# The recurrence's gate blocks in the two 64-row halves of the array, both directions side by side, in place of block-diagonal full blocks

## The chip, the cores and the metric

The kernel runs on one NeuronCore of one Trainium2 chip, as one launch. The metric is the device time of a run in microseconds (us), the median over runs: 1235.79 us for the kernel before (3 runs, 1235.56 to 1236.59). The four engines that compute are called PE (matrix multiply), DVE (vector), ACT (scalar, with table functions) and POOL; SP starts the transfers.

## What is computed

An encoder of two layers over 512 tokens of 1024 channels, all in float32. Each layer normalises its input, projects it with one matrix whose columns are split between eight attention heads (queries, keys, values), the input of a recurrence and its gate branch, joins the attention and the recurrence in an output projection, and ends in a gated MLP. The change touches the gates of the recurrence alone, which the reference writes so:

```python
def rg_lru(x, w_gate, b_gate, lam, reverse):
    bsz, s, _ = x.shape
    xb = x.reshape(bsz, s, N_LRU_BLOCKS, LRU_BLOCK)
    g = jnp.einsum("bsnc,gncd->gbsnd", xb, w_gate).reshape(2, bsz, s, D_LRU)
    g = g.astype(jnp.float32) + b_gate.astype(jnp.float32)[:, None, None, :]
    r_gate = jax.nn.sigmoid(g[0])
    i_gate = jax.nn.sigmoid(g[1])
    log_a = -LRU_C * r_gate * jax.nn.softplus(-lam.astype(jnp.float32))
    a = jnp.exp(log_a)
    u = jnp.sqrt(-jnp.expm1(2.0 * log_a)) * (i_gate * x.astype(jnp.float32))
    return linear_scan(a, u, reverse).astype(x.dtype)
```

There are 512 recurrent channels in 8 blocks of 64 (`N_LRU_BLOCKS`, `LRU_BLOCK`). For each of two directions `d` (forward, backward) and two gates `g` (0: `r_gate`, 1: `i_gate`), each block of 64 channels is multiplied by a 64 x 64 matrix of its own. Two scans along the tokens follow, one in each direction, whose results are added.

## The kernel before

Activations lie with channels on the 128 partitions and the 512 tokens along the row. Each float32 operand is split into a leading part (`h`, `hi`) and a trailing part (`l`, `lo`), and each product is three matmuls (`mm3`, L190 to L192: hi by h, hi by l, lo by h). The weights come as a stream of 205 chunks, each 128 x 1024 (eight blocks of 128 x 128), in the order in which PE takes them (`weight_plan`): SP starts the transfer into `raw`, ACT copies it into `hi` (L173), DVE subtracts to get `lo` (L174). Six chunks are loaded and three are split ahead of use; `hi` and `lo` have four buffers each.

Between the input of the recurrence and the output projection, `MIX` (L43) lists steps: query, key, value and gate-branch tiles (`qps`, `kps`, `vps`, `gate`: 24 matmuls each, from one chunk), the recurrence's convolution (`xc`, split into `xcs_h`, `xcs_l`) and its gates (`lru_gates`, steps t0 to t3), and the attention's scores (`s`), transposes (`ptw`, `pth`) and products (`o`). A scheduler then settles the order on each engine; an engine carries out its instructions in that order, and waits for what the next of them needs. Most of these products land in three banks of `ps_mm`, which are handed round: a product cannot start before the bank's former content has been read. `urgent()` puts the instructions that read a bank ahead of others in the scheduler's eyes.

`lru_gates` (L460) does one tile of 128 channels, four in a layer. For each direction and gate a 128 x 128 block with the two 64 x 64 matrices on its diagonal is multiplied with the tile (three matmuls 128x128x512 into a bank `gp`, whose digits after the name are layer, tile, direction and gate), and one tanh on ACT (L475) reads the whole bank, since sigmoid(z) is 0.5 + 0.5 tanh(z/2). So there are 12 matmuls, four banks and four tanhs a tile. For each direction follow exp, tanh and square on ACT (L478, L479, L481) and two products on DVE (L482, L483); then one square root over both directions (L487, with a load of ACT's function table before and after it), a product (L489), the two scans (L492 forward, L495 backward) and their sum (L497). The eight gate blocks of two tiles are one chunk, so a layer has two gate chunks, at t0 and t2.

Of the kernel before, what the change touches and what calls it, by code (L numbers as in the profile page):

```python
# [30 lines left out]
# query blocks of 8 grid columns: first key column, number of key columns, offset of the bias  # L31
# [3 lines left out]
# products that raise the tensor engine's clock while the first loads are under way  # L35
# [13 lines left out]
def weight_plan():  # L49
    """128 x 128 weight blocks in the order in which the tensor engine takes them, eight a chunk."""  # L50
    plan = []
    for l in range(L):
# [8 lines left out]
        for step in MIX:  # L61
            if step in ("t0", "t0a", "t2", "t2a"):
                t = int(step[1])
                plan.append(("gate", l, [(t + a, dg) for a in range(2) for dg in range(4)]))
            elif step[0] in IN_TILE and step[-1] != "b":
                column("w_in", IN_TILE[step[0]] + int(step[1]))
# [33 lines left out]
def encoder(ctx: ExitStack, tc: tile.TileContext, x_d, w_d, cols_d, bias_d, out_d):  # L100
# [93 lines left out]
    def gemm_group(banks, w, l, k0, nk, ms, rhs, hooks={}, first=0, total=None):  # L194
        """four tiles of the output at once, one step of the contraction after another"""
# [99 lines left out]
    class Stats:  # L295
# [13 lines left out]
        def columns(self, n, ps=None):  # L309
            """mean square + eps and its power of -1/2, token (128 s + p) at [p, s]"""  # L310
# [11 lines left out]
        def rows(self, c, pl=ps_mm):  # L322
            """the column c of token values on every partition"""
# [7 lines left out]
    # the token axis of the grid as columns of rows  # L331
# [9 lines left out]
    class Scaled:  # L341
        """x times a norm's gain, split; the norm's 1/rms is left to the products"""
# [16 lines left out]
    def finish(st, down_blk, h_in, r_in, l):  # L359
        """the last two tiles of the residual and the final norm, one half of the tokens after the other"""  # L360
# [58 lines left out]
    def layer(l, xn):  # L419
        # -- recurrent branch input --  # L420
# [34 lines left out]
        # -- recurrences --  # L455
# [5 lines left out]
        def lru_gates(t, ds):  # L461
            if t % 2 == 0 and 0 in ds:
                pair["c"] = chunk("gate", l, (t, 0))
            if 0 in ds:
                pair["w"], pair["work"] = p_w2.tile([P, 2 * T], F32, tag="w2", name=f"w2{l}{t}"), []
            c, both, work = pair["c"], pair["w"], pair["work"]
            for d in ds:
                w = both[:, d * T:(d + 1) * T]
                ti = big(p_t, "t", f"ti{l}{t}{d}")
# [13 lines left out]
                nc.vector.scalar_tensor_tensor(out=ti, in0=ti, scalar=1.0, in1=xc[t], op0=ALU.add, op1=ALU.mult)  # L483
                work.append((d, a, w, ti))
            if 1 not in ds:
                return
# [389 lines left out]
```

## Time and profile before

| what | value |
|---|---|
| median of 3 runs | 1235.79 us (1235.56 to 1236.59) |
| span of the profiled execution | 1234.5 us |
| PE busy | 1217.1 us (99%), 5694 instructions |
| DVE busy | 764.9 us (62%) |
| ACT busy | 481.8 us (39%) |
| granted TensorE clock | full in all 40 slices of the span |
| moved by DMA | 114.07 MB, mean 92 GB/s |

The durations and times of the trace come from one profiled execution, whose span is 1234.5 us; the median of the runs stands 1.3 us above it. Times within the trace count from the start of the span. The duration given for a matmul includes its way through the array: the pace is the distance between two starts. Matmuls of one kind follow each other while the former ones are still under way, so a "busy" PE may still be held up a little. The steps of `MIX` fall at about 40 to 165 us in layer 0 and 650 to 775 us in layer 1.

### The profile page before, as it was taken

How to read it: one execution, taken by the hardware profiler on the slowest of the kernel's cores; microseconds unless marked ns; L12 is line 12 of the kernel's file. 1: busy time of each engine (PE TensorE's matmuls, PEld its weight loads, DVE VectorE, ACT ScalarE, POOL GpSimd, SP SyncE). 2: the span in 40 equal slices, each digit the busy share in tenths (PEclk: the TensorE clock that was granted, in tenths of full speed). 3: DMA queues.
4: the chain of work that ended last, by engine and by line, in shares of the span. 5: the costliest groups of instructions: out<-in, count | busy, mean ns of one | idle time of the engine just before them, and what ended most of it. 6: DMA issues, size and time to landing. Idle time of an engine off the chain costs nothing.

```text
span 1234.5 us, 14411 instructions
## 1 busy us (share of the span) xinstructions
PE 1217.1 (99%) x5694; PEld 999.0 (81%) x5694; DVE 764.9 (62%) x1217; ACT 481.8 (39%) x701; POOL 23.7 (2%) x50
## 2 busy tenths in 40 slices
PE   9999999999999999999999999999999999999997
PEld 8777878888888888888887777788888888888886
DVE  7998756765544455554659977477555355555454
ACT  6676433432321232332428864344233222233220
POOL 2000000000000000000010000000000000000000
PEclk9999999999999999999999999999999999999999
DMA  7222213232332332333222221133323323323312
GB/s 259 62 86 90 76 42 103 85 103 91 97 103 94 95 102 91 97 103 96 91 85 76 76 86 52 35 122 101 99 90 103 102 87 101 102 87 102 102 52 69
DMA packets 34354, 114.07 MB, mean 92 GB/s; under 512 B 3824, under 2 KB 7024, under 8 KB 34288
## 3 DMA queue, kind: packets, MB, share of 16 engines
q1 hardware_dynamic: 34144, 113.17, 28.6%
q8 instruction: 44, 0.72, 0.2%
q14 instruction: 22, 0.18, 0.1%
q10 hardware_dynamic: 144, 0.00, 0.0%
HBM read 111.06 MB, written 2.10 MB: 92 GB/s over the span
## 4 chain that ended last, share of the span: by engine, by line
PE 93%; DVE 4%; issue 1%; DMA 0%; POOLq 0%; ACT 0%; POOL 0%; DVEq 0%; SPq 0%; ACTq 0%
PE dn L192 7%; PE dn L191 7%; PE dn L190 7%; PE pl L192 6%; PE pa L192 6%; PE pa L190 6%; PE pl L190 6%; PE pl L191 6%; PE pa L191 6%; PE out L190 2%; PE out L192 2%; PE out L191 2%; PE o L648 2%; PE o L653 2%; PE s L600 1%
## 5 line engine op out<-in xcount | busy, mean ns | idle before, releaser
L173 ACT ACTIVATE hi<-raw 128x1024 fp32r<-128x1024 f32 (+1 forms) x205 | 216.2, 1055 | 438.0 <-PE dn L191 158.9
L174 DVE TENSOR_TENSOR lo<-raw,hi 128x1024 fp32r<-128x1024 f32 (+1 forms) x205 | 249.2, 1216 | 138.0 <-ACT hi L173 137.9
L742 DVE TENSOR_TENSOR ua<-pa,g_ffn_rb 128x512 f32<-128x512 f32 x44 | 30.4, 691 | 112.8 <-PE pa L192 112.8
L750 ACT ACTIVATE uc<-uc,cols 128x512 f32<-128x512 f32 x48 | 34.8, 724 | 130.3 <-DVE uc L748 130.1
L751 DVE TENSOR_TENSOR uc<-pl,uc 128x512 f32<-128x512 f32 x44 | 30.4, 691 | 73.7 <-PE pl L192 72.0
L719 DVE TENSOR_TENSOR dns<-dn,g_ffn_rb 128x512 f32<-128x512 f32 x30 | 20.4, 688 | 29.5 <-PE dn L192 29.5
L748 DVE SCALAR_TENSOR_TENSOR uc<-ua,cols,uc 128x511 f32<-128x511 f32 x48 | 36.0, 751 | 1.6
L746 DVE SCALAR_TENSOR_TENSOR uc<-ua,cols,uc 128x511 f32<-128x511 f32 x48 | 35.8, 745 | 0.1
L612 ACT ACTIVATE p<-p,mx 128x192 f32<-128x192 f32 (+1 forms) x64 | 27.5, 431 | 16.6 <-DVE mx L610 16.6
L648 PE MATMUL o<-ptws,v 128*64 128x128 f32 x128 | 27.7, 298 | 0.0
L600 PE MATMUL s<-k,q 128*128 128x192 f32 (+1 forms) x128 | 23.0, 320 | 3.2 <-DVE q L520 2.2
L190 PE MATMUL out<-atth,hi 128*128 128x512 f32 x64 | 25.9, 405 | 0.0
L600 PEld LDWEIGHTS s<-k,q 128*128 128x128 f32 x128 | 19.9, 190 | 7.1 <-issue 4.3
L192 PE MATMUL out<-atth,lo 128*128 128x512 f32 x64 | 25.3, 395 | 0.0
L191 PE MATMUL out<-attl,hi 128*128 128x512 f32 x64 | 25.1, 392 | 0.0
L606 DVE CUSTOM_DVE_ANT_0 p<-s,bias 128x192 f32<-128x192 f32 (+1 forms) x64 | 18.3, 335 | 10.7 <-PE o L648 9.8
L745 DVE TENSOR_SCALAR uc<-ua,cols 128x512 f32<-128x512 f32 x48 | 23.4, 487 | 1.5
L520 DVE TENSOR_TENSOR q<-qps,g_mix_rb 64x256 f32<-64x256 f32 x32 | 20.6, 645 | 2.3 <-PE qps L192 1.8
L720 DVE TENSOR_TENSOR x<-x,dns 128x512 f32<-128x512 f32 x30 | 20.1, 687 | 0.4
L648 PEld LDWEIGHTS o<-ptws,v 128*64 128x64 f32 x128 | 12.2, 135 | 8.0 <-issue 3.9
L450 DVE SCALAR_TENSOR_TENSOR xc<-xrs,cols,xc 128x511 f32<-128x511 f32 (+1 forms) x24 | 17.9, 744 | 0.3
L192 PE MATMUL pl<-xg_g_ffn_4h,lo 128*128 128x512 f32 x44 | 17.1, 390 | 0.0
(918 smaller groups left out, 3475.2 us busy)
## 6 DMA issues: line engine op xcount, KB each, us to landing
raw<-in_w SPq DMA_DIRECT2D x203, 512.0 KB, 3.5
x<-in_x SPq DMA_DIRECT2D x8, 256.0 KB, 6.0
out_y<-out SPq DMA_DIRECT2D x8, 256.0 KB, 2.3
bias<-in_bias SPq DMA_DIRECT2D x8, 224.0 KB, 2.7
raw<-in_w SPq DMA_DIRECT2D x2, 256.0 KB, 3.6
cols<-in_cols SPq DMA_DIRECT2D x1, 164.0 KB, 6.7
cols<-in_cols ACTq DMA_DIRECT2D x1, 4.0 KB, 3.1
```

Source lines behind the costliest of these rows:

```text
L173: nc.scalar.activation(hi[:, sl], raw[:, sl], AF.Copy)
L174: nc.vector.tensor_tensor(out=lo[:, sl], in0=raw[:, sl], in1=f32(hi[:, sl]), op=ALU.subtract)
L190: nc.tensor.matmul(ps, a[0], b[0], start=start, stop=False)
L191: nc.tensor.matmul(ps, a[0], b[1], start=False, stop=False)
L192: nc.tensor.matmul(ps, a[1], b[0], start=False, stop=stop)
L600: nc.tensor.matmul(ps[:, o:o + ROWS * w], qt[:, b % 4 * P:(b % 4 + 1) * P], kt[:, ROWS * kc0:ROWS * (kc0 + w)], start=True, stop=True)
L648: nc.tensor.matmul(o[p0:p0 + 64, s * P:(s + 1) * P], v[i][:, s * P + p0:s * P + p0 + 64], by_head(t1)[:, 2 * (s % 2):2 * (s % 2) + 2, p0 / ...
L742: nc.vector.tensor_tensor(out=ua, in0=pa, in1=rbf[0], op=ALU.mult)
L746: nc.vector.scalar_tensor_tensor(out=c[:, 1:], in0=ua[:, :T - 1], scalar=w[0], in1=c[:, 1:], op0=ALU.mult, op1=ALU.add)
L748: nc.vector.scalar_tensor_tensor(out=c[:, :T - 1], in0=ua[:, 1:], scalar=w[2], in1=c[:, :T - 1], op0=ALU.mult, op1=ALU.add)
L750: nc.scalar.activation(c, c, AF.Gelu_apprx_tanh, bias=col("conv_ffn_b", j, l))
L751: nc.vector.tensor_tensor(out=c, in0=pl_, in1=c, op=ALU.mult)
```

## The change

The four block-diagonal blocks of a tile become two blocks, one for each gate. In such a block the rows 0 to 63 hold channel block s = 0 of the tile and the rows 64 to 127 hold s = 1, and the columns hold both directions side by side: 64 columns for one direction, 64 for the other (`o = 64 * (s ^ d)`). Each of the three products of a gate is now done twice, for the 64 rows of each half `n`, into a bank of its own (`gp` with layer, tile, gate and half as its digits): 12 matmuls a tile as before, each with 64 rows by 128 columns in place of 128 by 128, in the program's text alternating between the two halves.

A bank now holds both directions of one channel block, the forward direction in its own half of the partitions, the backward one in the other half. So each bank is read by two tanhs 64x512 (L485), eight a tile in place of four. All that belongs to the backward direction lies with its two halves swapped: `xc` is copied with swapped halves into `xs` (two copies 64x512 on ACT, L473), and the backward scan's result is copied back into place (two copies 64x512 on ACT, L510) before the sum. Biases and decays are packed to match on the host. The gate blocks of all four tiles of a layer fit in one chunk, which is taken at t0 and held until t3; the stream has 203 chunks in place of 205. The products on DVE stay as many.

```diff
-            if step in ("t0", "t0a", "t2", "t2a"):
-                t = int(step[1])
-                plan.append(("gate", l, [(t + a, dg) for a in range(2) for dg in range(4)]))
+            if step == "t0":
+                plan.append(("gate", l, [(t, g) for t in range(4) for g in range(2)]))
...
-                for g, o in ((0, w), (1, ti)):
-                    ps = psum(ps_o if d and g and not o_ps[0] else ps_mm, f"gp{l}{t}{d}{g}")
-                    mm3(ps, blk(c, 4 * (t % 2) + 2 * d + g), xcs[t], True, True)
...
+            xs = big(p_t, "t", f"xs{l}{t}")
+            halves_ = (slice(0, 64), slice(64, P))
+            for n in range(2):
+                nc.scalar.activation(xs[halves_[n]], xc[t][halves_[1 - n]], AF.Copy)
+            for g, o in ((0, ws), (1, ti)):
+                ps = [psum(ps_o if n and g and not o_ps[0] else ps_mm, f"gp{l}{t}{g}{n}") for n in range(2)]
+                w = blk(c, 2 * t + g)
+                for a, b in ((0, 0), (0, 1), (1, 0)):
+                    for n, rows in enumerate(halves_):
+                        nc.tensor.matmul(ps[n], w[a][rows], xcs[t][b][rows], start=a + b == 0, stop=a == 1)
+                for d in range(2):
                     i = ((l * 2 + d) * 2 + g) * 4 + t
                     with urgent():
-                        nc.scalar.activation(o, ps, AF.Tanh, scale=0.5, bias=half_b[:, i:i + 1])
+                        for n in range(2):
+                            rows = halves_[n ^ d]
+                            nc.scalar.activation(o[d][rows], ps[n][rows], AF.Tanh, scale=0.5, bias=half_b[rows, i:i + 1])
...
-                nc.vector.scalar_tensor_tensor(out=ti, in0=ti, scalar=1.0, in1=xc[t], op0=ALU.add, op1=ALU.mult)
-                work.append((d, a, w, ti))
...
+                nc.vector.scalar_tensor_tensor(out=ti[d], in0=ti[d], scalar=1.0, in1=xs if d else xc[t],
+                                               op0=ALU.add, op1=ALU.mult)
+                work.append((d, a, w, ti[d]))
...
-                    nc.vector.tensor_tensor(out=fb[t], in0=fb[t], in1=w, op=ALU.add)
+                    for n in range(2):
+                        nc.scalar.activation(u[halves_[n]], w[halves_[1 - n]], AF.Copy)
+                    nc.vector.tensor_tensor(out=fb[t], in0=fb[t], in1=u, op=ALU.add)
...
+            o = 64 * (s ^ d)
+            gate[:, :, :, 64 * s:64 * s + 64, o:o + 64] = a["lru_w"][:, d, :, s::2].transpose(0, 2, 1, 3, 4)
```

The scheduler orders the engines anew. In the rows below the numbers behind a name's letters are layer, tile and so on, and what follows the underscore only tells buffers apart. On ACT, in layer 0 around tile 2 of the gates, the order before is this (`p` is the softmax's exponential of scores, `w` and `ti` are the two gates, `w201` is that of tile 1):

```order
L173 ACTIVATE hi13_726<-raw13_695 128x1024
L487 ACT_TABLE_LOAD
L487 ACTIVATE w201_640<-w201_640 128x1024
L612 ACT_TABLE_LOAD
L612 ACTIVATE p034_1168,sm03_1166<-p034_1168,mx03_1165 128x192
L475 ACTIVATE w202_773<-gp0200_775,half_b_165 128x512
L475 ACTIVATE ti020_774<-gp0201_780,half_b_165 128x512
L612 ACTIVATE p034_1168,sm03_1166<-p034_1168,mx03_1165 128x192
L612 ACTIVATE p036_1174,sm03_1166<-p036_1174,mx03_1165 128x192
L475 ACTIVATE w202_773<-gp0210_793,half_b_165 128x512
L612 ACTIVATE p036_1174,sm03_1166<-p036_1174,mx03_1165 128x128
L173 ACTIVATE hi14_767<-raw14_730 128x1024
```

Here the first tanhs of tile 2 come between the exponentials, and the table load and the square root of tile 1 stand well ahead. The same place in the changed kernel:

```order
L626 ACTIVATE p034_1198,sm03_1196<-p034_1198,mx03_1195 128x192 x2
L626 ACTIVATE p036_1204,sm03_1196<-p036_1204,mx03_1195 128x192
L626 ACTIVATE p036_1204,sm03_1196<-p036_1204,mx03_1195 128x128
L499 ACT_TABLE_LOAD
L499 ACTIVATE w201_649<-w201_649 128x1024
L485 ACT_TABLE_LOAD
L485 ACTIVATE w202_785<-gp0200_791,half_b_165 64x512 x2
L485 ACTIVATE w202_785<-gp0201_792,half_b_165 64x512 x2
L510 ACTIVATE ti011_651<-w201_649 64x512 x2
L172 ACTIVATE hi13_744<-raw13_713 128x1024
L290 ACTIVATE xcs0_3h_781<-xc0_3_776 128x512
L473 ACTIVATE xs02_788<-xc0_2_640 64x512
```

All four exponentials, the square root of tile 1 and its two table loads now stand ahead of the first tanhs of tile 2, and behind these come the copies L510 and L473. On PE, in layer 0 where tile 3 of the gates is (`vps00` is the first value tile, `gate00` the first tile of the gate branch), the order before is this:

```order
L190 MATMUL gp0310_969<-xcs0_3h_763,hi11_597 128x512
L191 MATMUL gp0310_969<-xcs0_3l_764,hi11_597 128x512
L192 MATMUL gp0310_969<-xcs0_3h_763,lo11_598 128x512
L191 MATMUL vps00_917<-xg_g_mix0_5l_283,hi14_767 128x512
L192 MATMUL vps00_917<-xg_g_mix0_5h_282,lo14_768 128x512
L190 MATMUL vps00_917<-xg_g_mix0_6h_315,hi14_767 128x512
L191 MATMUL vps00_917<-xg_g_mix0_6l_316,hi14_767 128x512
L192 MATMUL vps00_917<-xg_g_mix0_6h_315,lo14_768 128x512
L190 MATMUL vps00_917<-xg_g_mix0_7h_322,hi14_767 128x512
L191 MATMUL vps00_917<-xg_g_mix0_7l_323,hi14_767 128x512
L192 MATMUL vps00_917<-xg_g_mix0_7h_322,lo14_768 128x512
L190 MATMUL gate00_1007<-xg_g_mix0_0h_170,hi15_818 128x512
```

The fourth bank of the gates, `gp0310`, is filled in the midst of the value tile, with seven of its matmuls between it and `gate00`. The same place in the changed kernel:

```order
L189 MATMUL vps00_938<-xg_g_mix0_7h_322,hi13_744 128x512
L190 MATMUL vps00_938<-xg_g_mix0_7l_323,hi13_744 128x512
L191 MATMUL vps00_938<-xg_g_mix0_7h_322,lo13_745 128x512
L479 MATMUL gp0310_988<-xcs0_3h_781,hi6_338 128x512
L479 MATMUL gp0310_988<-xcs0_3l_782,hi6_338 128x512
L479 MATMUL gp0310_988<-xcs0_3h_781,lo6_339 128x512
L189 MATMUL gate00_1037<-xg_g_mix0_0h_170,hi14_839 128x512
L190 MATMUL gate00_1037<-xg_g_mix0_0l_171,hi14_839 128x512
L191 MATMUL gate00_1037<-xg_g_mix0_0h_170,lo14_840 128x512
L189 MATMUL gate00_1037<-xg_g_mix0_1h_206,hi14_839 128x512
```

The last three gate matmuls, all in the lower half of the rows, now stand directly ahead of `gate00`, behind the whole value tile. On PE, in layer 1 behind tile 1 of the gates (`qps12` is a query tile, `ptw11` and `pth11` the transposes of the second half of a head pair's probabilities), the order before is this:

```order
L190 MATMUL qps12_5132<-xg_g_mix1_0h_4449,hi111_4949 128x512
L191 MATMUL qps12_5132<-xg_g_mix1_0l_4450,hi111_4949 128x512
L627 MATMUL ptw11_5531<-ident_158,p114_5490 128x128
L632 MATMUL pth11_5532<-ident_158,p114_5490 64x128
L627 MATMUL ptw11_5531<-ident_158,p114_5490 128x128
L632 MATMUL pth11_5532<-ident_158,p114_5490 64x128
L627 MATMUL ptw11_5531<-ident_158,p116_5496 128x128
L632 MATMUL pth11_5532<-ident_158,p116_5496 64x128
L627 MATMUL ptw11_5531<-ident_158,p116_5496 128x128
L192 MATMUL qps12_5132<-xg_g_mix1_0h_4449,lo111_4950 128x512
L190 MATMUL qps12_5132<-xg_g_mix1_1h_4458,hi111_4949 128x512
```

The transposes come after two matmuls of the query tile. The same place in the changed kernel:

```order
L191 MATMUL qps12_5180<-xg_g_mix1_5h_4620,lo110_4980 128x512
L641 MATMUL ptw11_5591<-ident_158,p114_5550 128x128
L646 MATMUL pth11_5592<-ident_158,p114_5550 64x128
L641 MATMUL ptw11_5591<-ident_158,p114_5550 128x128
L646 MATMUL pth11_5592<-ident_158,p114_5550 64x128
L641 MATMUL ptw11_5591<-ident_158,p116_5556 128x128 x2
L646 MATMUL pth11_5592<-ident_158,p116_5556 64x128
L189 MATMUL qps12_5180<-xg_g_mix1_6h_4679,hi110_4979 128x512
L190 MATMUL qps12_5180<-xg_g_mix1_6l_4680,hi110_4979 128x512
L191 MATMUL qps12_5180<-xg_g_mix1_6h_4679,lo110_4980 128x512
```

The transposes now come after 18 matmuls of the query tile.

## Rows read from the trace of the kernel before

**Rows 1.** The page, busy time of each engine.
```profile
PE 1217.1 (99%) x5694; PEld 999.0 (81%) x5694; DVE 764.9 (62%) x1217; ACT 481.8 (39%) x701; POOL 23.7 (2%) x50
```
**Rows 2.** The page, the chain that ended last, by engine.
```profile
PE 93%; DVE 4%; issue 1%; DMA 0%; POOLq 0%; ACT 0%; POOL 0%; DVEq 0%; SPq 0%; ACTq 0%
```
**Rows 3.** Waits of PE: us in total, times, longest.
```profile
PE ptw L627 <- DVE p L616: 3.5, 4, 1.5
PE s L600 <- DVE q L520: 2.2, 2, 1.6
```
**Rows 4.** Windows: us; busy (count) of each engine; PE clock; DMA share; GB/s.
```profile
40.00:125.00 85.00, 81.39 (x395) 64.25 (x395) 76.23 (x148) 65.75 (x107) 0.00 (x0) 1.00 0.26 80
125.00:165.00 40.00, 40.00 (x228) 31.07 (x228) 28.95 (x80) 18.21 (x44) 0.00 (x0) 1.00 0.20 65
650.00:735.00 85.00, 81.57 (x401) 65.34 (x401) 76.34 (x153) 65.67 (x110) 0.00 (x0) 1.00 0.26 83
```
**Rows 5.** Timeline of PE at gate tile 3, layer 0: start, us.
```profile
98.13 0.39 PE L190 MATMUL gp<-xcs_3h,hi 128*128 128x512 f32 x1
98.36 0.39 PE L191 MATMUL gp<-xcs_3l,hi 128*128 128x512 f32 x1
```
**Rows 6.** Operations on tiles named gp: ns min/median/max, first and last start, forms.
```profile
L190 PEld LDWEIGHTS gp<-xcs_0h,hi x8: 186/188/188, 40.1 to 650.1; 128*128 128x128 f32 x8
```
**Rows 7.** Timeline of PE, tiles of 64 rows between full ones.
```profile
111.98 0.39 PE L192 MATMUL gate<-xg_g_mix_7h,lo 128*128 128x512 f32 x1
112.30 0.43 PE L648 MATMUL o<-ptws,v 128*64 128x128 f32 x2
112.66 0.32 PE L653 MATMUL o<-pths,v 64*64 64x64 f32 x2
```
**Rows 8.** Groups of instructions on ACT: count, busy us, mean ns, idle before.
```profile
L173 ACT ACTIVATE hi<-raw 128x1024 fp32r<-128x1024 f32 x203 | 214.9, 1059 | 436.8 <-PE dn L191 158.9 <-PE pa L191 154.1 <-issue 30.7
L478 ACT ACTIVATE a<-w,spn 128x512 f32<-128x512 f32 x16 | 12.9, 807 | 0.0
L487 ACT ACT_TABLE_LOAD x8 | 10.3, 1283 | 0.1
```
**Rows 9.** Groups of instructions on DVE, the same columns.
```profile
L719 DVE TENSOR_TENSOR dns<-dn,g_ffn_rb 128x512 f32<-128x512 f32 x30 | 20.4, 688 | 29.5 <-PE dn L192 29.5
L636 DVE COPY pths<-pth 64x384 f32<-64x384 f32 x16 | 8.8, 548 | 8.0 <-PE pth L632 2.8 <-PE o L653 2.6 <-PE ptw L627 2.5
```
**Rows 10.** Timeline of ACT at gate tile 0, layer 0.
```profile
42.54 0.63 ACT L291 ACTIVATE xcs_1h<-xc 128x512 fp32r<-128x512 f32 x1 [0.61 <-DVE xc L450]
43.08 0.67 ACT L475 ACTIVATE ti<-gp,half_b 128x512 f32<-128x512 f32 x1
43.65 0.68 ACT L475 ACTIVATE w<-gp,half_b 128x512 f32<-128x512 f32 x1
```
**Rows 11.** Timeline of ACT at gate tile 2, layer 0.
```profile
79.42 1.28 ACT L612 ACT_TABLE_LOAD   x1 [0.71 <-DVE mx L610]
80.72 0.46 ACT L612 ACTIVATE p<-p,mx 128x192 f32<-128x192 f32 x1
81.23 0.69 ACT L475 ACTIVATE w<-gp,half_b 128x512 f32<-128x512 f32 x1
```
**Rows 12.** Timeline of PE, the starts that the walk compares.
```profile
84.51 0.40 PE L190 MATMUL kps<-xg_g_mix_0h,hi 128*128 128x512 f32 x1
103.57 0.39 PE L190 MATMUL gate<-xg_g_mix_0h,hi 128*128 128x512 f32 x1
673.30 0.33 PE L627 MATMUL ptw<-ident,p 128*128 128x128 f32 x1 [1.45 <-DVE p L616]
```
**Rows 13.** Timeline of DVE at gate tile 3, layer 0.
```profile
98.30 1.29 DVE L489 TENSOR_TENSOR ti<-ti,w 128x512 f32<-128x512 f32 x2
100.64 1.20 DVE L495 TENSOR_TENSOR_SCAN w<-a,ti 128x512 f32<-128x512 f32 x1
104.19 1.16 DVE L539 TENSOR_TENSOR vt<-vps,g_mix_rb 128x512 f32<-128x512 f32 x1
```

More of the change, by code (lines that the diff above doesn't have):

```diff
@@ L459, in layer, with lru_gates @@
         o_ps = [None]
[L461 to L469, printed above, removed]
-                for g, o in ((0, w), (1, ti)):
-                    ps = psum(ps_o if d and g and not o_ps[0] else ps_mm, f"gp{l}{t}{d}{g}")
-                    mm3(ps, blk(c, 4 * (t % 2) + 2 * d + g), xcs[t], True, True)
+        def lru_gates(t):
+            if t == 0:
+                pair["c"] = chunk("gate", l, (0, 0))
+            c = pair["c"]
+            both = p_w2.tile([P, 2 * T], F32, tag="w2", name=f"w2{l}{t}")
+            ws = [both[:, d * T:(d + 1) * T] for d in range(2)]
+            ti = [big(p_t, "t", f"ti{l}{t}{d}") for d in range(2)]
+            xs = big(p_t, "t", f"xs{l}{t}")
[9 more added lines that the diff above has]
+                for d in range(2):
                     i = ((l * 2 + d) * 2 + g) * 4 + t
                     with urgent():
-                        nc.scalar.activation(o, ps, AF.Tanh, scale=0.5, bias=half_b[:, i:i + 1])
+                        for n in range(2):
+                            rows = halves_[n ^ d]
+                            nc.scalar.activation(o[d][rows], ps[n][rows], AF.Tanh, scale=0.5, bias=half_b[rows, i:i + 1])
+            work = []
+            for d in range(2):
+                w = ws[d]
                 i = (l * 2 + d) * 4 + t
@@ L482, in lru_gates @@
                 nc.vector.scalar_tensor_tensor(out=w, in0=a2, scalar=1.0, in1=w, op0=ALU.add, op1=ALU.mult)
-                nc.vector.scalar_tensor_tensor(out=ti, in0=ti, scalar=1.0, in1=xc[t], op0=ALU.add, op1=ALU.mult)
-                work.append((d, a, w, ti))
-            if 1 not in ds:
-                return
+                nc.vector.scalar_tensor_tensor(out=ti[d], in0=ti[d], scalar=1.0, in1=xs if d else xc[t],
+                                               op0=ALU.add, op1=ALU.mult)
+                work.append((d, a, w, ti[d]))
             nc.scalar.activation(both, both, AF.Sqrt, scale=0.25)
-            for d, a, w, ti in work:
-                nc.vector.tensor_tensor(out=ti, in0=ti, in1=w, op=ALU.mult)
+            for d, a, w, u in work:
+                nc.vector.tensor_tensor(out=u, in0=u, in1=w, op=ALU.mult)
                 if d == 0:
                     fb[t] = big(p_fb, "fb", f"fb{l}{t}")
-                    nc.vector.tensor_tensor_scan(out=fb[t], data0=a, data1=ti, initial=0.0,
+                    nc.vector.tensor_tensor_scan(out=fb[t], data0=a, data1=u, initial=0.0,
                                                  op0=ALU.mult, op1=ALU.add)
                 else:
-                    nc.vector.tensor_tensor_scan(out=w[:, ::-1], data0=a[:, ::-1], data1=ti[:, ::-1], initial=0.0,
+                    nc.vector.tensor_tensor_scan(out=w[:, ::-1], data0=a[:, ::-1], data1=u[:, ::-1], initial=0.0,
                                                  op0=ALU.mult, op1=ALU.add)
-                    nc.vector.tensor_tensor(out=fb[t], in0=fb[t], in1=w, op=ALU.add)
+                    for n in range(2):
+                        nc.scalar.activation(u[halves_[n]], w[halves_[1 - n]], AF.Copy)
+                    nc.vector.tensor_tensor(out=fb[t], in0=fb[t], in1=u, op=ALU.add)
         qk = {}
@@ L691, in layer @@
             elif what == "t":
-                lru_gates(n, {"a": (0,), "b": (1,)}.get(step[-1], (0, 1)))
+                lru_gates(n)
             elif what == "n":
@@ L820, in lay_out @@
         blocks[n] = w.reshape(L, w.shape[1] // P, P, w.shape[2] // P, P).transpose(0, 1, 3, 2, 4)
-    gate = np.zeros((L, 4, 4, P, P), np.float32)
+    gate = np.empty((L, 4, 2, P, P), np.float32)
     for s in range(2):
         for d in range(2):
-            for g in range(2):
-                gate[:, :, 2 * d + g, 64 * s:64 * s + 64, 64 * s:64 * s + 64] = a["lru_w"][:, d, g, s::2]
+            o = 64 * (s ^ d)
+            gate[:, :, :, 64 * s:64 * s + 64, o:o + 64] = a["lru_w"][:, d, :, s::2].transpose(0, 2, 1, 3, 4)
     blocks["gate"] = gate
@@ L842, in lay_out @@
             put(COLS[n, l], a[n][l])
-    for n in ("lru_b", "lru_lam", "g_final"):
-        put(COLS[n], a[n])
+    lru = {}
+    for n in ("lru_b", "lru_lam"):
+        v = a[n].reshape(L, 2, -1, 2, 64).copy()
+        v[:, 1] = v[:, 1, :, ::-1]
+        lru[n] = v
+    for n, v in (("lru_b", lru["lru_b"]), ("lru_lam", lru["lru_lam"]), ("g_final", a["g_final"])):
+        put(COLS[n], v)
     rel = a["rel_bias"]
```

## The prediction

> **What bounds the kernel now.** I read the page first. PE is busy for 1217.1 of 1234.5 us, DVE for 764.9, ACT for 481.8 [rows 1], and the chain that ended last is PE for 93% and DVE for 4% [rows 2]. So the end is set by PE's work and by the few places where PE is held up. The list of PE's waits came next: of those that lie in the steps of `MIX`, transposes waiting for DVE's probabilities (3.5 us, the longest 1.5) and scores waiting for DVE's queries (2.2 us) are the largest [rows 3]. Then the windows, since a share over the whole span says nothing about a stage. In the two stretches with gates PE is busy 81.4 and 81.6 of 85 us, DVE 76, ACT 66: three engines near their limits, with 19.3 us of each stretch idle on ACT. In the 40 us behind the first, PE is busy for all of it [rows 4]: whatever PE is late by at the end of the gates, it stays late by, for nothing there waits that could give it back. What counts is thus (a) the time of the gate matmuls on PE and (b) the time by which ACT and DVE, with more to do, hand banks to PE later.
>
> **The gate matmuls on PE.** Both kernels have 96 of 512 columns. Before, each takes 98.36 − 98.13 = 0.23 us [rows 5], together 96 × 0.227 = 21.8 us. Afterwards each half-block has 64 rows. What a pair in two row halves costs no row shows, so I bound it. Below: the two run wholly beside each other, a pair in 0.227. Above: one after the other, 0.454. Nearest row: a weight load of 128 x 128 takes 188 ns [rows 6]; if the two loads of a pair follow each other on one path, a pair lasts at least 0.376. Not all 48 pairs can form: in tiles 0 and 3 of each layer the second gate's matmuls come three of one half and then three of the other, as the rows of the order at `gate00` show, and a third kind of break comes at tile 1 and 2 where other work lies between; by the order 35 pairs and 26 single ones are left. So the 96 take 61 × 0.227 = 13.8 us (a gain of 7.9), 35 × 0.376 + 26 × 0.227 = 19.1 (a gain of 2.7), or 21.8 (none). I take 19.1, being nearest to a row.
>
> The Trainium skill, page "TensorE: Matmul & The Clock Gate", Part 3 on packing small matmuls, says that tiles in different row groups run concurrently, and gives 3.07 times for four row tiles with 512 columns. No row of before shows two row halves beside each other. By that rule the gain would be nearer to the 7.9 than to the 2.7, and this is the last rival below.
>
> **Changing the shape.** Where a tile of 64 rows follows full ones, the first starts later: from 111.98 to 112.30 is 0.32 us in place of 0.227 [rows 7]. That is 0.09 us of draining, and the first load of the new shape can't hide behind the old one's matmuls: between nothing and 0.19 us more [rows 6], of which I take 0.11. So 0.2 us a switch. The order has the 96 matmuls in 15 contiguous blocks, each with one switch in and one out: 30 × 0.2 = +6.0 us. Bounds: nothing if the switch is free for these shapes; 0.05 a switch (half of the drain) would be 1.6; 6.0 is taken. PE's own sum is then 6.0 − 2.7 = +3.3 us, between −7.9 and +6.0. Most of it falls in the stretches where PE has 3.4 to 3.6 us of waits each [rows 4], 1.65 us a layer against 3.5: it takes the place of waiting, as long as ACT and DVE are what is late.
>
> **ACT's added work.** Per tile four more tanhs and four copies. The first question is what half the partitions cost. On DVE a copy of 64x384 takes 548 ns and a product of 128x512 688 ns [rows 9]: 384/512 of 688 would be 516, so the cost goes by the columns and not by the partitions. I carry that to ACT: bounds 0.28 (half) and 0.57 us, the distance of two tanhs 128x512 (43.65 − 43.08); a copy 0.53 to the next (43.08 − 42.54) [rows 10]. I take the full prices. A tile then costs 4 × 0.57 + 4 × 0.53 = 4.4 us more, a layer 17.6, less one split of 1.06 [rows 8] for the chunk that is gone: +16.5 us in a stretch where ACT has 19.3 idle. With the low price it is 4.4 for the tanhs and 4.2 for the copies, less 1.06: +7.6. DVE loses one subtraction a layer and gains nothing.
>
> The Trainium skill, page "TensorEngine Tiling (Array Packing)", section "PSUM Bottleneck", warns that tiling speeds up TensorE and not the emptying of PSUM. It speaks against this change; the trace agrees so far as each gate bank is read on ACT at 0.57 us, and there will be two reads a bank. The sums here do without it.
>
> **Where ACT's lateness meets PE.** ACT works in its order, and the banks of the gates come free by its tanhs. I walk layer 0. At tile 2, before, ACT begins a table load at 79.42 when DVE's maxima come, and the first tanh is at 81.23 [rows 11]; the key tile `kps` on PE starts at 84.51 [rows 12]. Now ahead of these tanhs stand four exponentials (0.51 each, 80.72 to 81.23: 2.0), a load 1.28, the square root 1.06, a load 1.28 [rows 8, 11], and the key tile needs two half-tanhs, 1.14. 79.42 + 6.8 = 86.2, so it starts 1.7 us later. From there ACT has, without a pause, two half-tanhs, two copies, split hi13, the split of `xcs`, a copy (4.4 in all, to 90.6), four half-tanhs and a copy (2.8), exp, tanh and square for two directions (six at some 0.67, between that 0.57 and the 0.81 that an exp lasts [rows 8]: 4.0) and two splits (2.1): 99.5; then a copy, a load and the square root: 102.4. On DVE the two products and two scans behind it took from 98.30 to 100.64 + 1.20 = 101.8 before [rows 13], 3.5 us: 105.9. Behind these, in DVE's order, stands the product `vt` that reads the value tile (1.16 us at 104.19 [rows 13]). Before, `gate` took another bank and began at 103.57 [rows 12], ahead of `vt`; now three banks are held by gate tile 3 and `gate00` takes the value tile's, so it waits for `vt` and starts at about 105.9 + 1.0 = 106.9: late by 3.3 us. As PE is full from there on, layer 0 ends 3.3 us later; the switches and the tile's pairs lie within these waits.
>
> In layer 1 the same chain would cost 3.3, but the transposes `ptw` that waited 1.45 us at 673.30 [rows 12] now come after 16 more matmuls, 3.6 us, so this wait goes; what is late next there is the bank of tile 2, on the same ACT. Bounds −1.45 (the wait goes, and the rest is as it was) and 3.3 (nothing gained); the scores' place shifts too, so I take 0.1, in the lower half. Sum: 3.3 + 0.1 = +3.4 us, a span of 1237.9; with 1.3 from the span to the median of the runs, 1239.2.
>
> **The rivals.**
> - *Row halves run one after the other.* PE's sum is +6.0, 3.0 a layer, nearly all of the waits it can hide in. For: no row shows an overlap. Against: the loads of 64-row products go on ahead too, two in 0.32 us [rows 7]. The lateness from ACT and a part of PE's own add up: taking 4.0 of the 6.0 as left bare and half of the 3.4 beside it, 1235.8 + 4.0 + 1.7 = 1241.5.
> - *ACT's work fits.* Half the partitions cost about half, or the tanhs, being urgent, are never far behind; ACT then has 66 + 8 = 74 of 85 us to do. Then banks come in time, the wait of `ptw` goes (−1.45), and PE's +3.3 lies half under waits (+1.65): about 1236. For: 19.3 us of idle time. Against: DVE's copy, and the order itself, which puts two table loads and a square root ahead of the tanhs of tile 2.
> - *Pairs overlap wholly and switches cost little*: −7.9 + 1.6 = −6.3 on PE, and ACT in time: 1229.5. It decides if the pairs start at intervals of 0.25 us or less and a block loses under 0.1. Against: the 188 ns loads, and ACT's order, which takes most of it back; half of the gain would be left, 1232.5.
> - *The change does less than it says*: the pairs are not made where the order has three and three; that is in the count of 35.
>
> **How the numbers follow.** A difference under 0.2%, 2.5 us, can't be told from none by a measurement of this kernel: 1233.3 to 1238.3 is the same. Forecast 1239.2, chance 0.45, its own range 1236.5 to 1242 from the half prices: 0.13 same, 0.32 slower. One after the other, 0.20: slower. ACT fits, 0.20: 0.14 same, 0.05 slower, 0.01 faster. Whole overlap, 0.15: 0.12 faster, 0.03 same. Together faster 0.13, same 0.30, slower 0.57. The range leaves out about 0.1 of the last rival below 1232.5 and 0.1 of the first above 1243.5.
>
> **What the profile afterwards would show.** Right: half-tanhs and half-copies at 0.5 us or more from one to the next; ACT busy for over 79 of the first 85 us; `gate` in layer 0 starting about 3 us later, with waits of PE for ACT's tanhs and DVE's `vt` in the list; no wait of `ptw` near 673. Pairs of gate matmuls starting under 0.1 us apart, a pair every 0.38, and some 0.2 us lost at each end of a block. Wrong: half-tanhs at 0.3 us, pairs every 0.23 us, or PE's waits no longer than before; then the time comes out below 1234. If gate matmuls start 0.23 us apart throughout, the first rival holds.

## The result

The changed kernel takes 1252.37 us (median of 4 runs, 1247.12 to 1253.59) against 1235.76 us before: a ratio of 1.0125, interval 1.0107 to 1.0143. It is slower, as forecast, by 16.6 us in place of 3.4, and lies outside the range. Its profiled execution, the longest of the four, has a span of 1251.8 us, 17.3 more than before. The page of the changed kernel (engines, granted clock in 40 slices, chain by engine):

```profile
PE 1224.2 (98%) x5694; PEld 996.9 (80%) x5694; DVE 764.5 (61%) x1215; ACT 521.9 (42%) x763; POOL 22.8 (2%) x50
...
PEclk9989999999999999999999989999999999999998
...
PE 87%; DVE 8%; ACT 3%; issue 2%; DMA 0%; SPq 0%; POOLq 0%; POOL 0%; DVEq 0%; ACTq 0%
```

PE's share of the chain fell from 93% to 87% [rows 2], and two slices in which the gates lie, from about 63 and 720 us, have lost clock. The windows of the changed kernel, the first three those of [rows 4], the last four cut out where the clock is low (the clock is the last but two):

```profile
40.00:125.00 85.00, 74.97 (x329) 56.47 (x328) 66.00 (x130) 73.65 (x122) 0.00 (x0) 0.92 0.22 68
125.00:165.00 40.00, 39.76 (x221) 30.92 (x221) 31.17 (x75) 24.91 (x51) 0.00 (x0) 1.00 0.20 61
650.00:735.00 85.00, 79.13 (x360) 60.44 (x358) 70.60 (x138) 72.72 (x122) 0.12 (x1) 0.96 0.21 63
...
45.20:48.60 3.40, 3.40 (x12) 2.72 (x10) 1.11 (x5) 3.12 (x6) 0.00 (x0) 0.50 0.42 141
65.60:72.40 6.80, 6.80 (x20) 4.24 (x19) 5.79 (x20) 4.75 (x8) 0.00 (x0) 0.50 0.00 0
113.40:116.80 3.40, 3.40 (x9) 2.65 (x9) 1.25 (x2) 3.33 (x6) 0.00 (x0) 0.50 0.00 0
721.00:727.80 6.80, 6.80 (x16) 4.44 (x16) 1.71 (x3) 6.73 (x8) 0.00 (x0) 0.50 0.54 154
```

The reader is to see the clock first: 1.00 in all these stretches before, and now four stretches, 20.4 us in all (20.5 by their exact ends), at the lower of its two levels, 1.2 in place of 2.4 GHz. In them PE works without a pause and does half as much, so they cost up to 10.2 us. Each begins behind a pause. Time and clock also go together from one execution to the next: the one of 1247.1 us had a mean granted clock of 0.994, the three of 1251.6 to 1253.6 had 0.988 to 0.990. PE's waits in the changed kernel, to be held beside [rows 3]:

```profile
PE gp L479 <- ACT w L485: 5.8, 3, 3.2
PE s L614 <- DVE q L534: 2.5, 2, 1.7
PE ptw L641 <- DVE p L630: 2.3, 4, 0.9
PE gp L479 <- DVE q L534: 2.1, 2, 1.6
...
PE kps L189 <- ACT w L485: 1.2, 1, 1.2
...
PE gate L189 <- DVE vt L553: 1.0, 1, 1.0
```

With three smaller ones (1.6) they make 16.5 us in the steps of `MIX`, where before there were about 7. The first is a new one, on ACT's tanhs, and 5.0 of its 5.8 us lie at tile 0 of the two layers. PE at that place in layer 0 and at `gate00`, then ACT of the changed kernel at both, and last ACT of the kernel before:

```profile
44.87 0.56 PE L479 MATMUL gp<-xcs_0h,hi 64*128 64x512 f32 x1 [3.18 <-ACT w L485]
45.23 0.62 PE L479 MATMUL gp<-xcs_0l,hi 64*128 64x512 f32 x1
45.66 0.62 PE L479 MATMUL gp<-xcs_0h,lo 64*128 64x512 f32 x1
...
113.14 0.57 PE L189 MATMUL gate<-xg_g_mix_0h,hi 128*128 128x512 f32 x1 [1.03 <-DVE vt L553]
```

```profile
42.92 0.63 ACT L290 ACTIVATE xcs_1h<-xc 128x512 fp32r<-128x512 f32 x1 [1.90 <-DVE xc L449]
43.46 2.64 ACT L485 ACTIVATE w<-gp,half_b 64x512 f32<-64x512 f32 x4
...
107.34 1.06 ACT L499 ACTIVATE w<-w 128x1024 f32<-128x1024 f32 x1
108.42 1.28 ACT L485 ACT_TABLE_LOAD   x1
109.71 2.66 ACT L485 ACTIVATE w<-gp,half_b 64x512 f32<-64x512 f32 x4
```

```profile
41.26 0.67 ACT L475 ACTIVATE w<-gp,half_b 128x512 f32<-128x512 f32 x1
```

ACT has the split of tile 1 (`xcs_1h`) ahead of the first tanhs and stands still 1.90 us for DVE's convolution; before, the order was the other way round, and the first tanh came at 41.26, ahead of the split of tile 1 at 42.54 [rows 10]. Then four half-tanhs take 2.64 us, 0.66 each. PE waits 3.18 us, and its next matmuls start 0.43 us apart (45.23 to 45.66) and not 0.23. At tile 3 (lower rows) ACT is later than the walk had it: the square root at 107.34, which the walk put at about 101.3, and the tanhs behind it. But up to 5 of these 6 us are owed to the clock, which was low for 10.2 us ahead of that place.

What the pairs and the switches cost is also to be read, from PE at tiles 0 and 2 of layer 0 of the changed kernel:

```profile
40.37 0.40 PE L479 MATMUL gp<-xcs_0l,hi 64*128 64x512 f32 x2
40.60 0.40 PE L479 MATMUL gp<-xcs_0h,lo 64*128 64x512 f32 x2
...
85.39 0.39 PE L191 MATMUL kps<-xg_g_mix_7h,lo 128*128 128x512 f32 x1
85.71 0.50 PE L479 MATMUL gp<-xcs_2h,hi 64*128 64x512 f32 x2
86.05 0.40 PE L479 MATMUL gp<-xcs_2l,hi 64*128 64x512 f32 x2
```

Two matmuls in two row halves are one row here (x2): they start 3 ns apart and run wholly beside each other, and the next pair starts 0.23 us later. The switch into the new shape takes 0.32 us in place of 0.227, and the first pair 0.34. The Trainium skill ("TensorE: Matmul & The Clock Gate", Part 3 on packing small matmuls) says that tiles in different row groups run concurrently, and the trace agrees.

### The profile page after: what moved, and what is told of

It reads as the page before. It is cut to its first block, busy times and chain, and to the rows that moved or that the text cites. A ratio compares the mean times of both kernels' runs of the same rounds, so it can differ in the third digit from the quotient of the medians.

```text
span 1251.8 us, 14498 instructions
## 1 busy us (share of the span) xinstructions
PE 1224.2 (98%) x5694; PEld 996.9 (80%) x5694; DVE 764.5 (61%) x1215; ACT 521.9 (42%) x763; POOL 22.8 (2%) x50
## 4 chain that ended last, share of the span: by engine, by line
PE 87%; DVE 8%; ACT 3%; issue 2%; DMA 0%; SPq 0%; POOLq 0%; POOL 0%; DVEq 0%; ACTq 0%
PE dn L190 7%; PE dn L189 7%; PE dn L191 7%; PE pa L190 6%; PE pl L190 6%; PE pl L191 6%; PE pa L191 6%; PE pa L189 6%; PE pl L189 6%; PE out L189 2%; PE out L191 2%; PE out L190 2%; PE o L662 2%; PE o L667 2%; DVE q L534 1%
## 5 line engine op out<-in xcount | busy, mean ns | idle before, releaser
L733 DVE TENSOR_TENSOR dns<-dn,g_ffn_rb 128x512 f32<-128x512 f32 x30 | 20.5, 689 | 29.4 <-PE dn L191 29.4
L485 ACT ACTIVATE ti<-gp,half_b 64x512 f32<-64x512 f32 x32 | 21.0, 679 | 0.8 <-DVE fb L504 0.2
L485 ACT ACTIVATE w<-gp,half_b 64x512 f32<-64x512 f32 x32 | 21.0, 677 | 0.7 <-PE gp L479 0.3
```

Of the source, the lines that this page charges most:

```text
L485: nc.scalar.activation(o[d][rows], ps[n][rows], AF.Tanh, scale=0.5, bias=half_b[rows, i:i + 1])
```

## The experiments

Times are medians, ratios to the kernel before in runs on the same chip (1235.7 to 1236.2 us). "Low" is the time at the lower clock in the steps of `MIX` in the profiled execution. The expectations speak of theories: A, that ACT's added work makes PE pause and the clock fall; B, that the row halves themselves bring it down; C, that a long pause alone does. The runs with the row halves alone, in turn or filled leave out the half-copies, and those with half the count leave out half of the gates' products.

| run | us | ratio (interval) | low, us |
|---|---|---|---|
| changed kernel | 1252.37 | 1.0125 (1.0107 to 1.0143) | 20.5 |
| ACT side alone | 1237.55 | 1.0012 (1.0002 to 1.0021) | 0 |
| row halves alone | 1242.11 | 1.0052 (1.0037 to 1.0067) | 10.2 |
| copies on POOL | 1254.63 | 1.0150 (1.0135 to 1.0166) | 23.9 |
| copies as transfers | 1245.91 | 1.0081 (1.0066 to 1.0096) | 10.2 |
| changed, split on DVE | 1253.88 | 1.0143 (1.0126 to 1.0160) | 17.1 |
| transfers, split on DVE | 1253.32 | 1.0139 (1.0123 to 1.0154) | 20.5 |
| row halves, split on DVE | 1242.83 | 1.0047 (1.0029 to 1.0065) | 10.2 |
| full rows, pause | 1235.60 | 0.9996 (0.9986 to 1.0005) | 0 |
| full rows, longer pause | 1241.08 | 1.0041 (1.0026 to 1.0056) | 3.4 |
| row halves in turn | 1239.44 | 1.0030 (1.0019 to 1.0040) | 6.8 |
| row halves, filled | 1253.62 | 1.0133 (1.0111 to 1.0154) | 10.2 |
| transfers, filled | 1263.66 | 1.0221 (1.0205 to 1.0237) | 13.7 |
| half the count, full rows | 1232.45 | 0.9970 (0.9959 to 0.9980) | 3.4 |
| the same with ACT's side | 1233.77 | 0.9979 (0.9970 to 0.9988) | 0 |

### ACT's side and the row halves apart

The ACT side alone keeps banks, half-tanhs and half-copies, and fills each bank with full blocks:

```diff
...
-                for a, b in ((0, 0), (0, 1), (1, 0)):
-                    for n, rows in enumerate(halves_):
-                        nc.tensor.matmul(ps[n], w[a][rows], xcs[t][b][rows], start=a + b == 0, stop=a == 1)
+                for n in range(2):
+                    mm3(ps[n], blk(c, 4 * (t % 2) + 2 * g + n), xcs[t], True, True)
...
```

> The ACT side of the change alone: banks, half-tanhs and half-copies as in the changed kernel, but each bank is filled by full 128 x 128 blocks (three matmuls, the other half of the rows being zero weights), so no row halves and no change of shape; two gate chunks a layer again. Theory A (the 64-partition tanhs and copies on ACT hold the banks, PE pauses, and the granted clock falls in the pauses): slower than before by 8 us or more, 1244 to 1258, with clock below 0.995. Theory B (the row halves themselves cost it, by switches of shape or by a clock that falls in them): 1234 to 1239, clock as before, 0.998.

The row halves alone keep the matmuls, read each bank with one tanh, and leave out the half-copies:

```diff
...
-                        for n in range(2):
-                            rows = halves_[n ^ d]
-                            nc.scalar.activation(o[d][rows], ps[n][rows], AF.Tanh, scale=0.5, bias=half_b[rows, i:i + 1])
+                        nc.scalar.activation(o[d], ps[d], AF.Tanh, scale=0.5, bias=half_b[:, i:i + 1])
...
```

> The row halves alone: the 12 matmuls of 64 rows a tile as in the changed kernel, but each bank is read by one tanh 128x512, four a tile, and the two swapped copies and the two copies back are left out (so the backward direction's second and first halves are not told apart). Theory A: faster than before, 1226 to 1234 (at most 7.9 us from the pairs, less the switches), clock 0.998. Theory B: 1246 or more, the clock low in the stages with gates as in the changed kernel.

Theory A alone fell at once: the ACT side comes out in Theory B's range. The row halves come out between the two ranges, slower than A has it and faster than B. Windows of the ACT side alone, with the start of `gate00` on its PE under them, and then windows of the row halves alone:

```profile
40.00:125.00 85.00, 82.36 (x397) 64.63 (x396) 73.43 (x147) 81.27 (x133) 0.00 (x0) 1.00 0.27 84
650.00:735.00 85.00, 81.34 (x390) 63.65 (x391) 71.13 (x146) 80.08 (x132) 0.00 (x0) 1.00 0.26 80
...
102.73 0.39 PE L190 MATMUL gate<-xg_g_mix_0h,hi 128*128 128x512 f32 x1
```

```profile
40.00:125.00 85.00, 79.89 (x376) 62.10 (x376) 73.31 (x142) 63.52 (x104) 0.00 (x0) 0.96 0.23 74
650.00:735.00 85.00, 78.81 (x376) 60.76 (x376) 72.89 (x140) 65.21 (x105) 0.00 (x0) 0.98 0.22 70
```

ACT is busy for 81 of 85 us in the first, as was forecast for the changed kernel, and yet the clock stays at 1.00 and the time at +0.12%. With row halves and ACT no busier than before, the clock falls and 6 us are lost. Neither part gives the 16.6 us, and their sum, 7.5, doesn't either; together they do.

### Copies moved off ACT

```diff
-                nc.scalar.activation(xs[halves_[n]], xc[t][halves_[1 - n]], AF.Copy)
+                nc.gpsimd.tensor_copy(xs[halves_[n]], xc[t][halves_[1 - n]])
...
-                        nc.scalar.activation(u[halves_[n]], w[halves_[1 - n]], AF.Copy)
+                        nc.gpsimd.tensor_copy(u[halves_[n]], w[halves_[1 - n]])
```

> The changed kernel with its four half-copies a tile on POOL in place of ACT; the eight half-tanhs stay. Theory A: between, 1236 to 1248, since half of ACT's added work is gone, if POOL's copies are not late themselves or slow DVE down. Theory B: as the changed kernel, 1247 to 1254.

The second has `nc.gpsimd.dma_start` in both places:

> The changed kernel with its four half-copies a tile as transfers within SBUF, started by POOL; the half-tanhs stay on ACT. Theory A: between, 1234 to 1246, ACT's added work being halved (2.6 us a tile in place of 5.2), and the copy back having time. Theory B: 1247 to 1254.

On POOL nothing is won (the clock is low for 23.9 us); as transfers 6.5 us come back, of which about 5 are the clock's: it is low for 10.2 us and not 20.5. The 1245.9 lies at the upper end of Theory A's range, below B's: beside row halves, ACT's added work does matter.

### The order at tile 0

The copy of tile 1 that stood ahead of the first tanhs goes to DVE:

```diff
-            xcs[t] = plain_split(p_h, "h", c, f"xcs{l}_{t}")
+            if t == 1:
+                xcs[t] = [big(p_h, "h", f"xcs{l}_{t}" + k, F32R) for k in "hl"]
+                nc.vector.tensor_copy(xcs[t][0], c)
+                nc.vector.tensor_tensor(out=xcs[t][1], in0=c, in1=f32(xcs[t][0]), op=ALU.subtract)
+            else:
+                xcs[t] = plain_split(p_h, "h", c, f"xcs{l}_{t}")
```

> The changed kernel with one instruction a layer on another engine: the copy that makes the leading part of tile 1 (xcs_1h), which stood on ACT ahead of the first tanhs of tile 0 and waited there for DVE's convolution, is done on DVE behind that convolution. Theory A (a pause of PE for banks that ACT holds, then a low clock for some us): PE's wait for the tanh near 42 to 45 us (3.2) shrinks to under 1.5, the clock doesn't fall there, and the time comes down by 2 to 8 us, 1244 to 1250. Theory B (the row halves bring the clock down whatever waits): 1250 to 1254, the clock still falling behind the gates of tile 0.

> Both changes: the four half-copies a tile as transfers within SBUF (as in the run before that had only these), and the leading part of tile 1 on DVE. In that earlier run the clock was low from 44.0 to 51.5 and 658.5 to 662.5 us. Theory A: these stretches go, worth (7.5 + 4.0) / 2 = 5.7 us, less up to 1.4 for DVE's added copy: 1238 to 1243, clock 0.997 or more. Theory B: 1244 to 1248.

> The row halves alone (one tanh 128x512 a bank, none of the half-copies, so the two directions' halves are not sorted), with the leading part of tile 1 on DVE. The run with the row halves alone had 1242.1, with a clock low from 43.5 to 51.0 and 654.5 to 658.5. Theory A: those stretches go: 1231 to 1238, clock 0.998. Theory B: 1241 to 1244, the clock as low as there.

None of the three gained; the transfers lost what they had won. The wait moved: in the changed kernel with the split on DVE, PE waits for DVE in place of ACT, and for ACT at tile 2 (3.0):

```profile
PE s L619 <- DVE k L547: 6.2, 4, 2.2
PE kps L189 <- ACT w L490: 3.3, 2, 3.0
```

The clock then falls behind other pauses, so the place of one pause isn't the cause. But not each pause brings a fall: one of the four executions of the row halves with the split on DVE kept its clock (mean 0.998) and took 1238.2 us, the other three (0.993 to 0.994) 1242.6 to 1243.4. That is also the plainest price of the clock, about 5 us in one and the same program. In the changed kernel itself tile 0 of layer 1 has nine 64-row matmuls and a pause of 1.85 us, and no fall behind it:

```profile
663.96 0.50 PE L479 MATMUL gp<-xcs_0h,hi 64*128 64x512 f32 x1 [1.85 <-ACT w L485]
...
663.90:670.70 6.80, 6.72 (x33) 5.51 (x34) 3.58 (x12) 6.71 (x14) 0.00 (x0) 1.00 0.24 77
```

### A pause with full rows

The kernel before, its first tanh made to wait for DVE's convolution of tile 1:

```diff
+                    if t == d == g == 0:
+                        hb = p_s.tile([P, 1], F32, tag="hb", name=f"hb{l}")
+                        nc.vector.scalar_tensor_tensor(out=hb, in0=xc[1][:, T - 1:T], scalar=0.0, in1=half_b[:, i:i + 1],
+                                                       op0=ALU.mult, op1=ALU.add)
```

> The kernel before, with full 128-row blocks, in which the first tanh of tile 0 of each layer is made to wait for DVE's convolution of tile 1 (its bias is made by a small DVE instruction that reads that convolution's last column, times zero). PE then pauses for a bank at the same place as in the changed kernel. Theory A: a pause near 42 to 45 us and a low clock for some us behind it though no matmul has 64 rows: 1238 to 1244, clock 0.990 to 0.996. Theory B: the pause of 1 to 3 us alone, clock 0.998, 1236 to 1239.

The longer one reads `xcs[1][1]` in place of `xc[1]`, for all four tanhs of tile 0:

> The kernel before with full blocks, in which all four first tanhs of tile 0 of each layer wait for DVE's trailing part of tile 1 (their biases are made behind it by small DVE instructions that read its last column, times zero), so that PE pauses longer than in the earlier run, about 3 to 4.5 us. Theory C (a long enough pause alone brings the clock down): low clock for 4 to 7.5 us behind it, 1240 to 1247, clock under 0.996. Theory B: the pause alone, 1237 to 1241, clock 0.998.

The first waits 1.7 us and loses nothing: 1235.6, clock full. The second has 2.93 us in layer 0 without a fall, and 2.32 us in layer 1 with one of 3.4 us:

```profile
45.04 0.49 PE L605 MATMUL s<-k,q 128*128 128x128 f32 x2 [2.93 <-DVE hb L477]
...
45.00:51.80 6.80, 6.76 (x37) 5.63 (x38) 3.49 (x19) 6.64 (x16) 0.00 (x0) 1.00 0.15 60
655.10:658.30 3.20, 3.20 (x10) 2.79 (x9) 1.41 (x8) 2.52 (x3) 0.00 (x0) 0.50 0.00 0
```

A long pause alone can do it, then; whether full rows bear more of it, one such pair doesn't tell, and the count below does better.

### Row halves in turn, and filled

In turn is the run with the row halves alone with the two loops around the matmul swapped; filled puts three full matmuls ahead of each gate's six, once there and once in the run with the transfers:

```diff
...
+                for _ in range(3):
+                    nc.tensor.matmul(ps[0], w[0], xcs[t][0], start=True, stop=True)
...
```

> The row halves alone (whole tanhs, no half-copies), with the three matmuls of one half ahead of the three of the other, so that nothing but the two at the border can run beside each other; PE's time for the gates is then about that of before plus the switches of shape. Theory C (the pairs' saved time becomes longer pauses, since DVE and ACT set the pace in these stages, and the clock falls after the long pauses): pauses as in the kernel before, the clock stays at 0.998, 1235 to 1240. Theory B (64-row matmuls bring the clock down, paired or not): low clock behind the gates as in the run with the row halves alone, 1241 to 1245.

> The row halves alone, paired, with three full 128-row matmuls 128x512 more ahead of each gate's six (into a bank that is then overwritten), which puts back the time that the pairs save, with full rows. Theory C: pauses and clock as in the kernel before, 1236 to 1241, clock 0.998. Theory B: the clock still falls behind the gates, 1241 to 1246.

> The changed kernel with its half-copies as transfers and the same three full-row matmuls ahead of each gate's six. The earlier run with the transfers alone: 1245.9, with a clock low from 44.0 to 51.5 and 658.5 to 662.5 us. Theory C: those stretches go, 1238 to 1242, clock 0.997 or more. Theory B: 1244 to 1249.

These three tell little. The scheduler made pairs of the first all the same, 31 as in the changed kernel. The fillers are 48 × 0.227 = 10.9 us, more than the 7.9 that the pairs save at most, the clock fell in both, and both times (1253.6 and 1263.7) lie above the ranges of either theory.

### The same time with full rows

Half of the gates' products are left out, so that three full matmuls take the time of three pairs; the run without ACT's side also makes the first tanhs of tile 0 wait for DVE's convolution:

```diff
...
-                for a, b in ((0, 0), (0, 1), (1, 0)):
-                    for n, rows in enumerate(halves_):
-                        nc.tensor.matmul(ps[n], w[a][rows], xcs[t][b][rows], start=a + b == 0, stop=a == 1)
+                nc.tensor.matmul(ps[0], w[0], xcs[t][0], start=True, stop=False)
+                nc.tensor.matmul(ps[1], w[0], xcs[t][0], start=True, stop=True)
+                nc.tensor.matmul(ps[0], w[1], xcs[t][1], start=False, stop=True)
...
```

> As the run with the row halves alone (whole tanhs, no half-copies, four banks), but each gate's six 64-row matmuls are three full 128-row ones, two into the first bank and one into the second (so half of the gates' products is left out): the time that the pairs take, without row halves and without a change of shape. The first tanhs of tile 0 are made to wait for DVE's convolution of tile 1 as they do there, so that PE pauses in the same place. Theory C (the pause alone): clock low near 44 to 51 and 654 to 658 us as there, 1236 to 1242. Theory B (the 64-row matmuls ahead of the pause are needed): clock 0.998, 1228 to 1236.

> The changed kernel with all its half-tanhs and half-copies on ACT, but each gate's six 64-row matmuls replaced by three full 128-row ones, two into the first bank and one into the second (half of the gates' products is left out). Theory C: pauses and falls of the clock much as in the changed kernel, 1243 to 1252. Theory B: few or no falls, and no switches of shape (6 us in all): 1233 to 1241.

Theory B's times both, though the clock of the first fell once, which B had not. With all of the changed kernel's work on ACT, and PE's gates as short as wholly paired halves, the time is 1233.8 and the clock doesn't fall in the gates: 18.6 us under the changed kernel. Windows of that run, and its ACT at tile 0:

```profile
40.00:125.00 85.00, 79.67 (x389) 62.97 (x388) 73.47 (x150) 81.15 (x133) 0.00 (x0) 1.00 0.23 74
650.00:735.00 85.00, 80.57 (x393) 63.08 (x392) 71.22 (x147) 80.46 (x137) 0.00 (x0) 1.00 0.22 71
...
40.95 2.64 ACT L485 ACTIVATE w<-gp,half_b 64x512 f32<-64x512 f32 x4
...
46.05 0.62 ACT L290 ACTIVATE xcs_1h<-xc 128x512 fp32r<-128x512 f32 x1
```

The 18.6 are not the clock's alone. In this run the order is another: the tanhs of tile 0 stand ahead of the split of tile 1, PE's pauses sum to 12 us and not 16.5, the longest is 1.5 and not 3.2, and there are no switches of shape.

The closest pair is tile 0 of layer 1. First PE and the window behind it in the run with the row halves alone, then in the one with half the count of full rows:

```profile
654.31 0.50 PE L476 MATMUL gp<-xcs_0h,hi 64*128 64x512 f32 x1 [1.16 <-ACT w L480]
...
655.00:658.20 3.20, 3.20 (x10) 2.42 (x9) 2.16 (x3) 2.66 (x4) 0.00 (x0) 0.50 0.41 164
```

```profile
648.91 0.50 PE L474 MATMUL gp<-xcs_0h,hi 128*128 128x512 f32 x1 [1.45 <-ACT w L485]
...
649.50:655.00 5.50, 5.42 (x29) 4.61 (x29) 4.21 (x13) 5.25 (x9) 0.00 (x0) 1.00 0.31 97
```

Behind nine 64-row matmuls a pause of 1.16 us is followed by half the clock; behind four full ones a pause of 1.45 us is not. In layer 0 the full rows lost the clock too, once, behind a pause of 2.50 us.

One pair proves little, as the 1.85 us without a fall shows. All of PE's pauses of 1 us or more in the steps of `MIX` can be counted, in the sixteen profiled executions, by whether a fall began in the pause or within 2.5 us of its end (one that began at the lower clock is left out):

| pause, us | full rows (6 kernels) | row halves (10 kernels) |
|---|---|---|
| 1 to 1.5 | 0 of 9 | 3 of 23 |
| 1.5 to 2 | 0 of 7 | 9 of 14 |
| 2 or more | 2 of 3 | 12 of 14 |

So pauses of like length were followed by falls more often in the kernels with row halves. The kernels are kin and their pauses not independent of each other. And the row halves need not stand right ahead: in the transfers with the split on DVE the clock fell at 118.6 and 142.4 us, behind pauses of 1.77 and 0.78, with no matmul into `gp` in the 3 us before.

## Why the prediction was wrong

The sign held; the size did not. Point by point:

- *Pairs.* The prediction took 0.376 us a pair, from two loads in a row. They take 0.23, and their loads run beside each other too. All 96 gate matmuls are in the records, and 31 pairs formed: a gain of 31 × 0.227 = 7.0, not 2.7 (7.9 with the 35 that were counted from the order). The first rival, one after the other, is out; the one with whole overlap was right in this price and furthest off in the time. Pairs every 0.23 us were also named as a sign that the time comes out below 1234, and it did not.
- *Switches.* 0.32 and 0.34 for two starts of 0.227, so 0.2 a switch, as predicted. The 15 blocks are there, and 30 switches are 6.0 us, less what lies within waits. (The 1.6 for 0.05 a switch should be 1.5.)
- *ACT's prices.* 0.66 us a half-tanh, above the upper bound of 0.57, and a half-copy as long as a whole one, 0.63. The rule (by columns, not partitions) held. But ACT was busy for 73.65 of the first 85 us and not over 79, since it waited too.
- *ACT's lateness.* The prediction gave it 3.4 us, and walked it to `gate00` at 106.9. The wait for `vt` at its end is there (1.03 us), but `gate00` started at 113.14, up to 5 us of it through the clock, and PE's longest wait is at tile 0, where the walk had none. With full rows and the same work on ACT, the whole costs 1.5 us (1237.55 against 1236.09), and `gate00` starts at 102.73, ahead of the 103.57 of [rows 12]: the order was another, and the tanhs came in time. So ACT's added work by itself is less than half of the term; in the changed kernel, with its order, PE's waits grew by 9.5.
- *"It takes the place of waiting"*: the step that failed. I set PE's time against the pauses as if exchanging the one for the other were free, with the clock at 1.00 throughout as in [rows 4]; no term of the sum and no rival had the clock. In fact PE's pauses grew by more than the forecast's whole 3.4 us, and behind many of the longer ones the clock halves. Summed for the profiled executions: pairs −7.0, switches at most +6.0, pauses 16.5 − 7.0 = +9.5, the clock 20.4 / 2 = +10.2; together at most +18.7 against 17.3 measured. The first two are counted, the last two read from the trace. For the row halves alone the clock is 10.2 / 2 = 5.1 of 6. So the sign came out right through a term that the forecast had, the waits, but that term was too small by about 6 us, and the largest one, the clock, stood at nothing.

How little there was to win shows in the two runs with ACT's side: 10.9 us fewer of full-row matmuls (half of 21.8) took 3.8 us off the time (1237.55 to 1233.77).

The Trainium skill ("TensorE: Matmul & The Clock Gate", section "A second HAM failure mode: psum-queue depth-cycling") describes PE idling a little between groups of matmuls as it goes from bank to bank, and paying with the clock. The trace agrees in three of the changed kernel's four falls: the waits of 3.18, 1.03 and 1.6 us ahead of them are for banks that ACT or DVE still reads, and the clock is at 0.50 behind them. The fourth is behind a wait for DVE's queries.

What stays open: why the clock falls more often in the kernels with row halves. The count shows that it does, at pauses of like length; no run has the same pauses in the same places with the shape alone changed. Nor do the runs part the 64 rows as such from the running of two halves beside each other, since the run meant for that was paired too. Part of the pauses comes from the order that the scheduler gave the changed kernel, above all at tile 0, and no run has the changed kernel with the whole order of the full rows.

## What to carry to other kernels

Time saved on PE in a stage where other engines set the pace can end as a pause, and a pause can cost more than it saved: ask of each stretch what the clock was, and what PE did ahead of it. Half-array matmuls that run in pairs took half the time here, but the kernels with them had the clock at its lower level for three to seven microseconds at a time; try the same time with full rows before blaming the waits. And a half-partition instruction on ACT costs as much as a whole one or more, so a layout that needs two for one is paid in full.

## What was not expected of the hardware

- Four half-tanhs 64x512 in a row took 2.64 us, 0.66 each, against 0.57 from one whole tanh to the next [rows 10].
- Weight loads of the two row halves ran beside each other as the matmuls did: a pair every 0.23 us, its two loads 3 ns apart, although one load takes 0.188 [rows 6].
- Of PE's pauses of 1.5 us or more, 21 of 28 were followed by 1.2 GHz in the kernels with row halves, and 2 of 10 in those with full rows. Single pauses go either way: 1.16 us behind 64-row matmuls was followed by it, 1.85 us behind them and 2.93 us behind full ones were not.
- A copy of 64x512 from one half of the partitions to the other as a transfer started by POOL landed 2.3 us later, and taking four of these a tile off ACT gave back 6.5 us of 16.6.
